# HGRN2's intra-chunk levels 1 to 32: products over the odd-block positions only, one masked copy per level, masks stored as bytes

## Chip, cores and metric

The kernel runs on one core of a Trainium2 chip. The metric is the device time of one execution in microseconds, as the median of several runs; less is better.

## What is computed

One decoder layer over 1024 prompt positions and 32 sampled positions (8 sequences of 4): RMS norm, one input projection, two mixers side by side (four mLSTM heads and four HGRN2 heads of 128 x 128), an output projection, a SwiGLU feed-forward block and a final norm. The change lies in the HGRN2 mixer, whose reference is

```
def _hgrn_chunk(S, inp):
    q, k, lf, v = inp
    b = jnp.cumsum(lf, axis=2)
    inter = jnp.einsum('bhtk,bhkv->bhtv', q * jnp.exp(b), S)
    dec = jnp.exp(jnp.where(mask[:, :, None], b[:, :, :, None, :] - b[:, :, None, :, :], -jnp.inf))
    A = jnp.einsum('bhtk,bhsk,bhtsk->bhts', q, k, dec)
    o = inter + jnp.einsum('bhts,bhsv->bhtv', A, v)
    S_new = jnp.exp(bL[:, :, 0, :])[..., None] * S + jnp.einsum('bhsk,bhsv->bhkv', k * jnp.exp(bL - b), v)
```

The matrix A couples a later position t with an earlier position s through a product of per-channel forget factors between them. The kernel works with chunks of 128 positions and builds A by levels, so that no quotient of factors is needed.

## The kernel before

**Stages.** The 1056 positions are cut into three blocks (288, 384 and 384 columns; the first holds 256 prompt positions and the 32 sampled ones). For each weight tile the input projection runs over the blocks: a unit is eight k-steps of three matmuls (`emit_k`, L135 to L137: high part times high part, low times high, high times low, with operands rounded for the fast matmul). Four units make one head of one block: first all mLSTM heads, then all HGRN2 heads, then the output projection and the feed-forward part.

**Order.** The program is written under a manual schedule: each engine executes its instructions in the order in which the Python code issues them, and semaphores hold an instruction until its inputs are there. Mixers are generators; `hook()` is called after every second k-step of a unit and lets each active generator run to its next `yield`, whose number says how many hooks to skip. So the mixer's small matmuls stand between k-steps of the projection on TensorE (PE), and its elementwise work stands in the queues of VectorE (DVE), ScalarE (ACT) and GpSimd (POOL) between the evacuation of projection results and the splitting of weights (L96 on ACT, L97 on POOL).

**One HGRN2 head of one block** is `mix_b(h, b)`: twelve times in all, with two chunks in block 0 and three in blocks 1 and 2. Channels lie on the partitions, positions along the free axis. `q`, `k` and the forget factors `f` are fp32 tiles (`cq`, `ck`, `ngb`); `qp` (tile `qw`) starts as q times f.

- Diagonal: one 128 x 128 product per chunk (`prod`, L757) goes to a PSUM bank; four multiplications by the identity, one per quadrant of 32 partitions (L772), copy the diagonal into AT, the tile that holds A transposed (s on the partitions, t along the free axis, one 128-column slice per chunk).
- Levels 1, 2, 4, 8, 16, 32, 64: at level l, t lies in the odd block of l positions and s in the even block before it. The products of `k` and `qp` are taken (levels 1 to 16: the whole 128 x 128 product per chunk, L757; level 32: two 32 x 32 products per chunk, L788; level 64: one 64 x 64 product, L793), then the odd blocks of `qp` are multiplied by the factors of the even block (DVE, L801), the even blocks of `k` by those of the odd block (POOL, L802), and pairs of factors are combined for the next level (DVE, L806). The wanted entries are copied out of PSUM: levels 1 to 8 by four masked copies of 32 partitions each (L813), level 16 by four plain copies (L821), levels 32 and 64 by ScalarE (L825, L827).
- Then k and v are transposed, the state is advanced, and AT times v and `qp` times the state make the output.

Block 0 also has the 32 sampled positions of the head: products of 32 x 32 (L759) at the diagonal and at levels 1 and 2, copied into tile PB (L776, L818). They use one quarter of the PE array's columns (`tile_position`).

AT is one of two tiles used in turn. The mLSTM gates of block 0 use the same two tiles as scratch, and `gates_sample` fills them with zeros on POOL when it is done (L391). The masks are part of the constant input: `cst` arrives as fp32 by one DMA on ACT's queue (L1615), and DVE converts the 64 mask columns to bytes (L1678) into tile `msk`.

An fp32 product is executed as two passes, each a weight load (PEld) and a matmul (PE) in the trace: 160 products of L757 in the levels show as 320 rows.

Of the kernel before, what the change touches and what calls it, by code (L numbers as in the profile page):

```python
# [9 lines left out]
F32 = mybir.dt.float32  # L10
F32R = mybir.dt.float32r
U8 = mybir.dt.uint8
AF = mybir.ActivationFunctionType
OP = mybir.AluOpType

D = 1024
T = 1056
# [14 lines left out]
NPLAIN = 2  # L32
EPS = 1e-6
QS = 128 ** -0.5
LEVELS = [1, 2, 4, 8]

V_G1, V_G2, V_GF, V_BIN, V_BG, V_CW, V_CB, V_MN, V_HN, V_LB, NV = 0, 8, 16, 24, 56, 57, 89, 97, 101, 105, 113

# [2 lines left out]
def hybrid_step(ctx: ExitStack, tc: tile.TileContext, i, o):  # L41
    nc = tc.nc
# [5 lines left out]
    mp = p1.enter_context(tc.tile_pool(name="mixp", bufs=1))  # L48
# [99 lines left out]

    vec = cn.tile([128, NV], F32, name="vec")
    ident = cn.tile([128, 128], F32, name="ident")  # L150
    cst = mp.tile([128, 232], F32, name="cst")
    msk = mp.tile([128, 64], U8, name="msk")
    X = act.tile([128, KT, T], F32, tag="X", name="X")
    x2 = [X]
    HI = act.tile([128, KT * T], F32R, name="HI")
# [22 lines left out]
    load_x(0)  # L178
    nc.scalar.dma_start(vec, i["vec"])
    maskneg, seqm, mneg4 = cst[:, 0:128], cst[:, 128:136], cst[:, 136:168]  # L180
    mk = {1: msk[:, 0:16], 2: msk[:, 16:32], 4: msk[:, 32:48], 8: msk[:, 48:64]}
    nc.scalar.preload_act_table_set("sqrt_and_others")
    ones = cn.tile([128, 1], F32, name="ones")
    nc.vector.memset(ones, 1.0)
# [168 lines left out]
    def gates_sample(ig, lf):  # L353
        def t5(name):
            return mp.tile([4, 40], F32, tag=name, name=name)

        def v5(x):
            return x.rearrange("p (s t) -> p s t", t=5)

        def s4(x):  # L360
            return x[:, 256:288].rearrange("p (s t) -> p s t", t=4)
        lfe, ige, rm, Fe, me = (t5(x) for x in ("lfe", "ige", "rme", "Fe", "me"))
        nc.vector.memset(lfe, -1e30)
        nc.vector.memset(rm, 1.0)
# [12 lines left out]
        nc.vector.tensor_tensor(wi, ng, m0s[:, :, None].to_broadcast([4, 8, 4]), op=OP.add)  # L377
        nc.scalar.activation(wi, wi, AF.Exp)
        nc.vector.tensor_tensor(wl, g, ng[:, :, 3:4].to_broadcast([4, 8, 4]), op=OP.add)
        nc.scalar.activation(wl, wl, AF.Exp)  # L380
        yield 2
        mo = mp.tile([4, 8], F32, tag="mso", name="mso")
        nc.vector.tensor_copy(mo[:, :, None], m4[:, :, 3:4])
        nc.sync.dma_start(o["ms"], mo)
        nc.sync.dma_start(d_sc.rearrange("j h t -> h j t"), r[:, 0:3].rearrange("p j s t -> p j (s t)"))
        nc.sync.dma_start(d_bc[:, 0, 256:288], ng.rearrange("p s t -> p (s t)"))
        nc.sync.dma_start(d_bc[:, 1, 256:288], wi.rearrange("p s t -> p (s t)"))
        for j in range(3):
            nc.sync.dma_start(scol[:, j:j + 1], d_sc[j].rearrange("h t -> (h t)")[:, None])
        for a in ATs:  # L390
            nc.gpsimd.memset(a, 0.0)  # L391

    def bc_row(row, n):
        return bass.AP(tensor=row.tensor, offset=row.offset, ap=[[0, 128], [1, n]])
# [201 lines left out]
    PB = mp.tile([128, 128], F32, name="PB")  # L596
# [148 lines left out]
    def mix_b(h, b):  # L745
        ncb, npr, n = NCH[b], NPR[b], BL[b]
        q, f, k = S["qb", h, b], S["f", h, b], S["kb", h, b]
        AT = ATs[atn[0] % 2]
# [5 lines left out]
        def prod(ps, a, c_, lo=0):  # L754
            for c in range(ncb):
                s = slice(c * 128, c * 128 + 128)
                nc.tensor.matmul(ps[:, s], a[:, s], c_[:, s], start=True, stop=True)  # L757
            if lo:
                nc.tensor.matmul(ps[32 * h:32 * h + 32, 256:288], a[:, 256:288], c_[:, 256:288], start=True, stop=True,  # L759
                                 tile_position=(0, 32 * h))  # L760

        def quads(fn):
            for j in range(4):
                fn(slice(32 * j, 32 * j + 32))
        hs = slice(32 * h, 32 * h + 32)
        nc.gpsimd.tensor_tensor(qp[:, :n], q[:, :n], f[:, :n], op=OP.mult)
        yield 2
        ps = bank()
        prod(ps, k, q, samp)

        def dg(js):
            nc.vector.tensor_tensor(AT[js, :ncb, js], ps[js, :npr].rearrange("p (c t) -> p c t", t=128)[:, :, js],  # L772
                                    ident[js, None, js].to_broadcast([32, ncb, 32]), op=OP.mult)
        quads(dg)
        if samp:
            nc.vector.tensor_tensor(PB[hs, hs], ps[hs, 256:288], ident[hs, hs], op=OP.mult)  # L776
        yield 2
# [1 line left out]
        while lv < 128:  # L779
            sm = samp and lv <= 2  # L780
            nn = n if sm else npr
            ps = bank()
            if lv <= 16:
                prod(ps, k, qp, sm)
            elif lv == 32:
                for c in range(ncb):
                    for s0 in (0, 64):
                        nc.tensor.matmul(ps[s0:s0 + 32, c * 128:c * 128 + 32], k[:, c * 128 + s0:c * 128 + s0 + 32],  # L788
                                         qp[:, c * 128 + s0 + 32:c * 128 + s0 + 64], start=True, stop=True,
                                         tile_position=(0, s0))  # L790
            else:
                for c in range(ncb):
                    nc.tensor.matmul(ps[0:64, c * 128:c * 128 + 64], k[:, c * 128:c * 128 + 64],  # L793
                                     qp[:, c * 128 + 64:c * 128 + 128], start=True, stop=True)
            nb = nn // (2 * lv)

# [7 lines left out]
            if lv == 4:  # L804
                go2 = go + nn // lv
            nc.vector.tensor_tensor(gx[:, go2:go2 + nb, None], gv[:, :, 0:1], gv[:, :, 1:2], op=OP.mult)  # L806
            pc = ps[:, :npr].rearrange("p (c t) -> p c t", t=128)
            if lv <= 8:
                def ext(js):
                    src = pc[js, :, js].rearrange("p c (n two l) -> p c n two l", two=2, l=lv)[:, :, :, 1, :]  # L810
                    dst = AT[js, :ncb, js].rearrange("p c (n two l) -> p c n two l", two=2, l=lv)[:, :, :, 1, :]
                    m = mk[lv][js].rearrange("p (n l) -> p n l", l=lv)
                    nc.vector.copy_predicated(dst, m[:, None].to_broadcast([32, ncb, 16 // lv, lv]), src)  # L813
                quads(ext)
                if sm:
                    src = ps[hs, 256:288].rearrange("p (n two l) -> p n two l", two=2, l=lv)[:, :, 1, :]
                    dst = PB[hs, hs].rearrange("p (n two l) -> p n two l", two=2, l=lv)[:, :, 1, :]
                    nc.vector.copy_predicated(dst, mk[lv][hs].rearrange("p (n l) -> p n l", l=lv), src)  # L818
            elif lv == 16:
                for j in range(4):  # L820
                    nc.vector.tensor_copy(AT[32 * j:32 * j + 16, :ncb, 32 * j + 16:32 * j + 32],  # L821
                                          pc[32 * j:32 * j + 16, :, 32 * j + 16:32 * j + 32])
            elif lv == 32:
                for s0 in (0, 64):
                    nc.scalar.activation(AT[s0:s0 + 32, :ncb, s0 + 32:s0 + 64], pc[s0:s0 + 32, :, 0:32], AF.Copy)  # L825
            else:
                nc.scalar.activation(AT[0:64, :ncb, 64:128], pc[0:64, :, 0:64], AF.Copy)  # L827
            if samp and lv == 2:
# [783 lines left out]

    load(0)
    nc.scalar.dma_start(ident, i["cst"][:, 0:128])
    nc.scalar.dma_start(cst, i["cst"][:, 128:360])  # L1615
    load(1)
    load(2)
    load_x(1)
# [56 lines left out]
    start(startup(1), ("n1", 1))  # L1675
    start(startup(2), ("n1", 2))
    hook()
    nc.vector.tensor_copy(msk, cst[:, 168:232])  # L1678
    nxt = 2
    b0_first = 3 + 12 * H  # L1680
    def next_splits(ui):
# [156 lines left out]

def _constants():
    p = np.arange(128)  # L1840
    cst = np.zeros((128, 360), np.float32)
    cst[:, 0:128] = np.eye(128)
    cst[:, 128:256] = np.where(p[:, None] <= p[None, :], 0.0, -1e30)
    cst[:, 256:264] = (p[:, None] % 32) // 4 == np.arange(8)[None, :]
    s, t = (p % 32)[:, None], np.arange(32)[None, :]
    cst[:, 264:296] = np.where((s // 4 == t // 4) & (s <= t), 0.0, -1e30)
    msk = cst[:, 296:360]
    r = p % 32
    for j, l in enumerate(LEVELS):
        n = np.arange(16) // l  # L1850
        msk[:, 16 * j:16 * j + 16] = ((r[:, None] // (2 * l)) == n[None, :]) & ((r[:, None] % (2 * l)) < l)
    return cst


def _prepare(x):
# [3 lines left out]
    def tiles(w):  # L1859
# [19 lines left out]
    xp = x["x_prompt"].reshape(1024, 1024)  # L1879
    xall = np.concatenate([xp[:256], x["x_sample"].reshape(32, 1024), xp[256:]], axis=0)  # L1880
    wgu = np.stack([tiles(x["w_gate"][0]), tiles(x["w_up"][0])], axis=1).reshape(44, 128, 1024)
    cst = _constants()
    return {
        "xT": xall.T.reshape(8, 128, T).transpose(1, 0, 2), "vec": vec, "cst": cst,
        "wA": wA, "wo": tiles(x["w_out"][0]), "wgu": wgu, "wd": x["w_down"][0],
        "hist": x["state_conv"][0].reshape(8, 3, 8, 128).transpose(3, 2, 0, 1).reshape(128, 8, 24),
        "C0": x["state_mlstm_C"][0], "n0T": x["state_mlstm_n"][0].transpose(2, 0, 1).reshape(128, 32),
# [28 lines left out]
```

## Time and profile before

| | |
|---|---|
| median of 3 runs | 1446.07 us (1445.78 to 1446.92) |
| the profiled execution's own time | 1442.34 us |
| its span | 1440.5 us |
| PE busy | 1366.2 us, 95% of the span |
| PE weight loads busy | 1334.2 us, 93% |
| DVE, ACT, POOL busy | 930.2 us (65%), 523.5 us (36%), 636.8 us (44%) |
| HGRN2 stage, from the first diagonal product to the last level | about 306 to 592 us of the span |

How to read it. The span is divided into stages whose limits differ, so the shares of the whole say little about one stage. PE is pipelined: a matmul's row lasts longer than the distance to the next one's start, and what a matmul costs in a dense stream is the distance from start to start. A row of the timeline that stands for several instructions (x6) begins with the first and ends with the last of them. An idle time in square brackets is the engine's, just before the row, with what ended it.

### The profile page before, as it was taken

Reading aid. Unit: us, or ns where it says so; the run is one execution under the profiler, and the core shown is the slowest. Engines: PE = TensorE matmul, PEld = TensorE weight load, DVE = VectorE, ACT = ScalarE, POOL = GpSimd, SP = SyncE. Lnnn points to the kernel's source line nnn. Section 1 sums busy time; section 2 is a strip of 40 time slices with the busy share of each in tenths; the row PEclk is TensorE's granted clock in tenths of the full one; section 3 lists DMA queues with packets and bytes.
Section 4 is the critical chain, followed back from the end, with each engine's and each line's share of the span. In section 5 each row is a group of like instructions: output and inputs, shape, how many; then the busy total and the mean of one; then the engine's idle time right before and its main releaser. Section 6 shows DMA issues by size and latency. Waiting matters only on the chain. (4 is left out here: it accounts for less than half of the span.)

```text
span 1440.5 us, 27183 instructions
## 1 busy us (share of the span) xinstructions
PE 1366.2 (95%) x10384; PEld 1334.2 (93%) x10384; DVE 930.2 (65%) x2192; ACT 523.5 (36%) x1195; POOL 636.8 (44%) x648
## 2 busy tenths in 40 slices
PE   7879999999999998999988998999999999999996
PEld 6779999999999998899988998999999999999995
DVE  7876657666777768744564655656555436777776
ACT  6554434322222223322434443444444441222232
POOL 5313213234343435222436654556545674544435
PEclk8999999999999999999999999999999999999998
DMA  6012212420101113553454655666565358887843
GB/s 218 23 42 76 65 37 73 123 80 30 33 30 32 45 32 112 144 155 105 158 196 146 217 210 167 216 220 220 193 212 186 124 190 333 291 298 277 300 157 121
DMA packets 108875, 211.97 MB, mean 147 GB/s; under 512 B 10800, under 2 KB 63560, under 8 KB 108232
## 3 DMA queue, kind: packets, MB, share of 16 engines
q1 hardware_dynamic: 108312, 209.98, 42.9%
q8 instruction: 82, 1.34, 0.4%
q14 instruction: 49, 0.40, 0.1%
q10 hardware_dynamic: 432, 0.24, 0.1%
HBM read 143.73 MB, written 66.45 MB: 146 GB/s over the span
## 5 line engine op out<-in xcount | busy, mean ns | idle before, releaser
L135 PE MATMUL mm<-HI,whi 128*128 128x384 f32 (+2 forms) x1160 | 381.9, 329 | 6.9 <-ACT gA L302 2.9
L136 PE MATMUL mm<-LO,whi 128*128 128x384 f32 (+2 forms) x1160 | 363.4, 313 | 0.9 <-POOL LO L225 0.4
L137 PE MATMUL mm<-HI,wlo 128*128 128x384 f32 (+2 forms) x1160 | 363.0, 313 | 1.3 <-POOL wlo L97 1.3
L135 PEld LDWEIGHTS mm<-HI,whi 128*128 128x128 f32 x1160 | 221.7, 191 | 12.0 <-ACT gA L302 3.2
L136 PEld LDWEIGHTS mm<-LO,whi 128*128 128x128 f32 x1160 | 221.9, 191 | 2.1 <-POOL LO L225 0.9
L137 PEld LDWEIGHTS mm<-HI,wlo 128*128 128x128 f32 x1160 | 221.5, 191 | 1.8 <-POOL wlo L97 1.8
L97 POOL TENSOR_TENSOR wlo<-raw,whi 128x512 fp32r<-128x512 f32 x90 | 119.8, 1340 | 143.8 <-ACT whi L96 98.8
L1365 DVE TENSOR_TENSOR fh<-fr,fh 128x512 fp32r<-128x512 f32 x80 | 71.6, 894 | 129.4 <-ACT fh L1364 129.3
L1157 POOL TENSOR_TENSOR wlo<-S,whi 128x512 fp32r<-128x512 f32 x78 | 103.2, 1328 | 115.9 <-ACT whi L1156 109.0
L1228 PE MATMUL mx<-T,whi 128*128 128x264 f32 x640 | 122.6, 290 | 12.4 <-DVE sg L1195 6.3
L1228 PEld LDWEIGHTS mx<-T,whi 128*128 128x128 f32 x640 | 101.7, 193 | 14.1 <-DVE sg L1195 7.3
L1281 POOL TENSOR_TENSOR LO<-rg,HI 128x528 fp32r<-128x528 f32 x52 | 70.5, 1365 | 65.7 <-ACT HI L1280 65.7
L1228 PE MATMUL mx<-HI,whi 128*128 128x264 f32 x320 | 91.7, 287 | 4.8 <-ACT u L1236 4.8
L1228 PE MATMUL mx<-T,wlo 128*128 128x264 f32 x320 | 92.3, 288 | 0.0
L1228 PE MATMUL mx<-HI,wlo 128*128 128x264 f32 x320 | 90.9, 284 | 0.0
L1228 PE MATMUL mx<-LO,whi 128*128 128x264 f32 x320 | 90.7, 284 | 0.0
L802 POOL TENSOR_TENSOR ck<-ck,wib 128x192 f32<-128x192 f32 (+2 forms) x72 | 41.3, 574 | 99.6 <-PE mx L757 56.1
L1156 ACT ACTIVATE whi<-S 128x512 fp32r<-128x512 f32 x80 | 50.4, 632 | 95.4 <-DVE S L1145 95.4
L1446 DVE TENSOR_TENSOR X<-X,mx 128x264 f32<-128x264 f32 x160 | 65.3, 424 | 27.1 <-PE mx L1442 26.6
L1364 ACT ACTIVATE fh<-fr 128x512 fp32r<-128x512 f32 x80 | 45.6, 572 | 71.5 <-issue 31.4
L1280 ACT ACTIVATE HI<-rg 128x528 fp32r<-128x528 f32 x52 | 32.3, 641 | 105.7 <-PE mx L1442 32.8
L1228 PE MATMUL mm<-HI,wlo 128*128 128x264 f32 x240 | 68.2, 284 | 0.0
(536 smaller groups left out, 3580.0 us busy)
## 6 DMA issues: line engine op xcount, KB each, us to landing
d_wf<-fh SPq DMA_DIRECT2D x60, 512.0 KB
rg<-d_ff SPq DMA_DIRECT2D x42, 528.0 KB
raw<-in_wA SPq DMA_DIRECT2D x31, 512.0 KB
whi<-d_wf SPq DMA_DIRECT2D x29, 512.0 KB
wlo<-d_wf SPq DMA_DIRECT2D x28, 512.0 KB
raw<-in_wgu SPq DMA_DIRECT2D x24, 512.0 KB
d_ff<-sg SPq DMA_DIRECT2D x40, 264.0 KB
rg<-in_wgu SPq DMA_DIRECT2D x20, 512.0 KB
```

The source lines that it names most:

```text
L97: (nc.gpsimd if pool else nc.vector).tensor_tensor(lo[:, s], raw[:, s], hi[:, s].bitcast(F32), op=OP.subtract)
L135: nc.tensor.matmul(ps[:, :n], wh, rh[:, k, :], start=(k == 0), stop=False)
L136: nc.tensor.matmul(ps[:, :n], wh, rl[:, k, :], start=False, stop=False)
L137: nc.tensor.matmul(ps[:, :n], wl, rh[:, k, :], start=False, stop=(k == nk - 1))
L802: nc.gpsimd.tensor_tensor(ke, ke, gv[:, :, 1:2].to_broadcast([128, nb, lv]), op=OP.mult)
L1156: nc.scalar.activation(hi[:, s], t, AF.Copy)
L1157: (nc.vector if dve else nc.gpsimd).tensor_tensor(lo[:, s], t, hi[:, s].bitcast(F32), op=OP.subtract)
L1228: nc.tensor.matmul(ps[:, :QN], a[:, w], b_[:, kk, c], start=new and kk == 0 and x == 0, stop=kk == 3 and x == 2, skip_group_check=True)
L1281: (nc.vector if dve else nc.gpsimd).tensor_tensor(lw, src, h.bitcast(F32), op=OP.subtract)
L1364: nc.scalar.activation(h, src, AF.Copy)
L1365: nc.vector.tensor_tensor(lw, src, h.bitcast(F32), op=OP.subtract)
L1446: nc.vector.tensor_tensor(y, y, ps[:, :QN], op=OP.add)
```

## The change

At levels 1 to 32 the moving operand of the product holds only the 64 positions of a chunk that lie in odd blocks (`odd(qp, l)`: runs of l positions with gaps of l), against all 128 columns of `k`, so each product is 128 x 64 and a level's result fills 64 columns per chunk in PSUM without gaps. At levels 1 to 16 one masked copy over 128 partitions and 64 positions per chunk takes the entries (level 16 now with a mask too); the diagonal is one multiplication over the whole 128 x 128 tile, which also writes the zeros, and so the fill of the two AT tiles goes. Level 32 has one product per chunk in place of two small ones; ScalarE copies as before, from other columns. Level 64 differs only in where its result lies in PSUM. The masks are 64 columns for each of the five levels, come as bytes by a DMA of their own on ACT's queue, and the conversion on DVE goes.

```diff
-LEVELS = [1, 2, 4, 8]
+LEVELS = [1, 2, 4, 8, 16]
...
-    cst = mp.tile([128, 232], F32, name="cst")
-    msk = mp.tile([128, 64], U8, name="msk")
+    cst = mp.tile([128, 168], F32, name="cst")
+    msk = mp.tile([128, 320], U8, name="msk")
...
-        for a in ATs:
-            nc.gpsimd.memset(a, 0.0)
...
-        def quads(fn):
-            for j in range(4):
-                fn(slice(32 * j, 32 * j + 32))
+        def odd(x, l):
+            return x.rearrange("p (n two l) -> p n two l", two=2, l=l)[:, :, 1, :]
+
+        def prod_odd(ps, l, lo):
+
+            for c in range(ncb):
+                s = slice(c * 128, c * 128 + 128)
+                nc.tensor.matmul(ps[:, 64 * c:64 * c + 64].rearrange("p (n l) -> p n l", l=l), k[:, s], odd(qp[:, s], l),
+                                 start=True, stop=True)
+            if lo:
+                nc.tensor.matmul(ps[32 * h:32 * h + 32, 256:288], k[:, 256:288], qp[:, 256:288], start=True, stop=True,
+                                 tile_position=(0, 32 * h))
...
-        def dg(js):
-            nc.vector.tensor_tensor(AT[js, :ncb, js], ps[js, :npr].rearrange("p (c t) -> p c t", t=128)[:, :, js],
-                                    ident[js, None, js].to_broadcast([32, ncb, 32]), op=OP.mult)
-        quads(dg)
+        nc.vector.tensor_tensor(AT[:, :ncb, :], ps[:, :npr].rearrange("p (c t) -> p c t", t=128),
+                                ident[:, None, :].to_broadcast([128, ncb, 128]), op=OP.mult)
...
-            if lv <= 16:
-                prod(ps, k, qp, sm)
-            elif lv == 32:
-                for c in range(ncb):
-                    for s0 in (0, 64):
-                        nc.tensor.matmul(ps[s0:s0 + 32, c * 128:c * 128 + 32], k[:, c * 128 + s0:c * 128 + s0 + 32],
-                                         qp[:, c * 128 + s0 + 32:c * 128 + s0 + 64], start=True, stop=True,
-                                         tile_position=(0, s0))
+            if lv <= 32:
+                prod_odd(ps, lv, sm)
...
-            if lv <= 8:
-                def ext(js):
-                    src = pc[js, :, js].rearrange("p c (n two l) -> p c n two l", two=2, l=lv)[:, :, :, 1, :]
-                    dst = AT[js, :ncb, js].rearrange("p c (n two l) -> p c n two l", two=2, l=lv)[:, :, :, 1, :]
-                    m = mk[lv][js].rearrange("p (n l) -> p n l", l=lv)
-                    nc.vector.copy_predicated(dst, m[:, None].to_broadcast([32, ncb, 16 // lv, lv]), src)
-                quads(ext)
+            if lv <= 16:
+                dst = AT[:, :ncb, :].rearrange("p c (n two l) -> p c n two l", two=2, l=lv)[:, :, :, 1, :]
+                m = mk[lv].rearrange("p (n l) -> p n l", l=lv)
+                nc.vector.copy_predicated(dst, m[:, None].to_broadcast([128, ncb, 64 // lv, lv]),
+                                          pc.rearrange("p c (n l) -> p c n l", l=lv))
...
-            elif lv == 16:
-                for j in range(4):
-                    nc.vector.tensor_copy(AT[32 * j:32 * j + 16, :ncb, 32 * j + 16:32 * j + 32],
-                                          pc[32 * j:32 * j + 16, :, 32 * j + 16:32 * j + 32])
...
-    nc.scalar.dma_start(cst, i["cst"][:, 128:360])
+    nc.scalar.dma_start(cst, i["cst"][:, 128:296])
+    nc.scalar.dma_start(msk, i["msk"])
...
-    nc.vector.tensor_copy(msk, cst[:, 168:232])
```

No other instruction changes its place on its engine.

## Rows read from the trace of the kernel before

**Rows 1.** Windows: stretch, length, busy us (instructions) of PE, PEld, DVE, ACT, POOL, clock, DMA

```profile
306.00:592.00 286.00, 279.60 (x2077) 266.36 (x2076) 209.28 (x651) 78.55 (x213) 119.23 (x165) 1.00 0.17 50
```

**Rows 2.** Timeline of PE around one level's six passes: start us, duration us, instruction

```profile
331.58 0.34 PE L137 MATMUL mm<-HI,wlo 128*128 128x384 f32 x1
331.75 0.83 PE L757 MATMUL mx<-qw,ck 128*128 128x128 f32 x6
...
332.60 0.34 PE L136 MATMUL mm<-LO,whi 128*128 128x384 f32 x1
```

**Rows 3.** Timeline of PE around six passes with one moving column (a norm's sums)

```profile
36.01 0.29 PE L137 MATMUL mx<-HI,wlo 128*128 128x288 f32 x1
36.14 0.73 PE L207 MATMUL mx<-ones,vt 128*128 128x1 f32 x6
...
36.94 0.29 PE L136 MATMUL mx<-LO,whi 128*128 128x288 f32 x1
```

**Rows 4.** Timeline of PE around level 32 of a three-chunk block

```profile
346.47 0.34 PE L137 MATMUL mm<-HI,wlo 128*128 128x384 f32 x1
346.74 0.38 PE L788 MATMUL mx<-qw,ck 128*32 128x32 f32 x12
...
347.33 0.34 PE L136 MATMUL mm<-LO,whi 128*128 128x384 f32 x1
```

**Rows 5.** Timeline of PE at level 2 of block 0, head 0

```profile
312.60 0.61 PE L757 MATMUL mx<-qw,ck 128*128 128x128 f32 x4
313.14 0.25 PE L759 MATMUL mx<-qw,ck 128*32 128x32 f32 x2
```

**Rows 6.** DVE groups by shape, 306 to 596 us: count, busy us, mean ns, idle before

```profile
L813 DVE COPY_PREDICATED AT<-msk,mx 32x48 f32<-32x48 uint8 x128 | 29.7, 232 | 3.2
L813 DVE COPY_PREDICATED AT<-msk,mx 32x32 f32<-32x32 uint8 x64 | 13.1, 205 | 1.5
L772 DVE TENSOR_TENSOR AT<-mx,ident 32x96 f32<-32x96 f32 x32 | 8.1, 254 | 12.8 <-PE mx L757 12.0
L821 DVE COPY AT<-mx 16x48 f32<-16x48 f32 x32 | 6.5, 202 | 0.7
L848 DVE COPY kt<-mx 128x384 f32<-128x384 f32 x7 | 3.9, 558 | 0.2
```

**Rows 7.** Timeline of PE, 550 to 593 us: rows with idle time before them

```profile
557.41 0.38 PE L788 MATMUL mx<-qw,ck 128*32 128x32 f32 x12 [1.97 <-DVE wib L806]
564.43 0.43 PE L672 MATMUL so<-st,qz 128*32 128x128 f32 x8 [1.81 <-DMA st<-in_S]
583.32 0.43 PE L672 MATMUL so<-st,qz 128*32 128x128 f32 x8 [0.43 <-POOL qz L633]
585.46 0.94 PE L757 MATMUL mx<-qw,ck 128*128 128x128 f32 x6 [0.42 <-POOL ck L802]
591.38 0.56 PE L793 MATMUL mx<-qw,ck 128*64 128x64 f32 x6 [0.97 <-POOL ck L802]
```

**Rows 8.** Timeline of DVE ahead of the first of these waits

```profile
550.86 0.93 DVE L813 COPY_PREDICATED AT<-msk,mx 32x48 f32<-32x48 uint8 x4
...
555.25 1.42 DVE L741 TENSOR_SCALAR ngb<-ngb,omlb,lb 128x384 f32<-128x384 f32 x1
```

**Rows 9.** Timeline of POOL ahead of the waits at 583 and 591 us

```profile
581.44 1.40 POOL L498 TENSOR_TENSOR sm<-sm,mhalf 128x3 f32<-128x3 f32 x1 [1.19 <-DVE sm L493]
...
590.10 0.60 POOL L498 TENSOR_TENSOR sm<-sm,mhalf 128x1 f32<-128x1 f32 x1 [2.56 <-DVE sm L493]
```

**Rows 10.** Timeline of DVE at the start of the program

```profile
27.01 1.26 DVE L1678 CAST msk<-cst 128x64 uint8<-128x64 f32 x1
...
31.31 1.22 DVE L1637 TENSOR_TENSOR vt<-vt,qw 128x384 f32<-128x384 f32 x2
32.64 3.02 DVE L1637 TENSOR_TENSOR vt<-vt,go 128x384 f32<-128x384 f32 x2
```

**Rows 11.** Page, part 3, DMA queue: packets, MB, share of 16 engines

```profile
q1 hardware_dynamic: 108312, 209.98, 42.9%
```

More of the change, by code (lines that the diff above doesn't have):

```diff
@@ L180, in hybrid_step @@
     maskneg, seqm, mneg4 = cst[:, 0:128], cst[:, 128:136], cst[:, 136:168]
-    mk = {1: msk[:, 0:16], 2: msk[:, 16:32], 4: msk[:, 32:48], 8: msk[:, 48:64]}
+    mk = {l: msk[:, 64 * j:64 * j + 64] for j, l in enumerate(LEVELS)}
     nc.scalar.preload_act_table_set("sqrt_and_others")
@@ L782, in mix_b @@
             ps = bank()
-            if lv <= 16:
-                prod(ps, k, qp, sm)
-            elif lv == 32:
-                for c in range(ncb):
-                    for s0 in (0, 64):
-                        nc.tensor.matmul(ps[s0:s0 + 32, c * 128:c * 128 + 32], k[:, c * 128 + s0:c * 128 + s0 + 32],
-                                         qp[:, c * 128 + s0 + 32:c * 128 + s0 + 64], start=True, stop=True,
-                                         tile_position=(0, s0))
+            if lv <= 32:
+                prod_odd(ps, lv, sm)
             else:
                 for c in range(ncb):
-                    nc.tensor.matmul(ps[0:64, c * 128:c * 128 + 64], k[:, c * 128:c * 128 + 64],
+                    nc.tensor.matmul(ps[0:64, c * 64:c * 64 + 64], k[:, c * 128:c * 128 + 64],
                                      qp[:, c * 128 + 64:c * 128 + 128], start=True, stop=True)
@@ L806, in mix_b @@
             nc.vector.tensor_tensor(gx[:, go2:go2 + nb, None], gv[:, :, 0:1], gv[:, :, 1:2], op=OP.mult)
-            pc = ps[:, :npr].rearrange("p (c t) -> p c t", t=128)
-            if lv <= 8:
-                def ext(js):
-                    src = pc[js, :, js].rearrange("p c (n two l) -> p c n two l", two=2, l=lv)[:, :, :, 1, :]
-                    dst = AT[js, :ncb, js].rearrange("p c (n two l) -> p c n two l", two=2, l=lv)[:, :, :, 1, :]
-                    m = mk[lv][js].rearrange("p (n l) -> p n l", l=lv)
-                    nc.vector.copy_predicated(dst, m[:, None].to_broadcast([32, ncb, 16 // lv, lv]), src)
-                quads(ext)
-                if sm:
-                    src = ps[hs, 256:288].rearrange("p (n two l) -> p n two l", two=2, l=lv)[:, :, 1, :]
-                    dst = PB[hs, hs].rearrange("p (n two l) -> p n two l", two=2, l=lv)[:, :, 1, :]
-                    nc.vector.copy_predicated(dst, mk[lv][hs].rearrange("p (n l) -> p n l", l=lv), src)
-            elif lv == 16:
-                for j in range(4):
-                    nc.vector.tensor_copy(AT[32 * j:32 * j + 16, :ncb, 32 * j + 16:32 * j + 32],
-                                          pc[32 * j:32 * j + 16, :, 32 * j + 16:32 * j + 32])
+            pc = ps[:, :64 * ncb].rearrange("p (c t) -> p c t", t=64)
+            if lv <= 16:
[3 more added lines that the diff above has]
+                                          pc.rearrange("p c (n l) -> p c n l", l=lv))
+                if sm:
+                    nc.vector.copy_predicated(odd(PB[hs, hs], lv),
+                                              mk[lv][hs, 16 * h:16 * h + 16].rearrange("p (n l) -> p n l", l=lv),
+                                              odd(ps[hs, 256:288], lv))
             elif lv == 32:
                 for s0 in (0, 64):
-                    nc.scalar.activation(AT[s0:s0 + 32, :ncb, s0 + 32:s0 + 64], pc[s0:s0 + 32, :, 0:32], AF.Copy)
+                    nc.scalar.activation(AT[s0:s0 + 32, :ncb, s0 + 32:s0 + 64], pc[s0:s0 + 32, :, s0 // 2:s0 // 2 + 32],
+                                         AF.Copy)
             else:
@@ L1840, in _constants @@
     p = np.arange(128)
-    cst = np.zeros((128, 360), np.float32)
+    cst = np.zeros((128, 296), np.float32)
     cst[:, 0:128] = np.eye(128)
@@ L1846, in _constants @@
     cst[:, 264:296] = np.where((s // 4 == t // 4) & (s <= t), 0.0, -1e30)
-    msk = cst[:, 296:360]
-    r = p % 32
+    msk = np.zeros((128, 64 * len(LEVELS)), np.uint8)
     for j, l in enumerate(LEVELS):
-        n = np.arange(16) // l
-        msk[:, 16 * j:16 * j + 16] = ((r[:, None] // (2 * l)) == n[None, :]) & ((r[:, None] % (2 * l)) < l)
-    return cst
+        n = np.arange(64) // l
+        msk[:, 64 * j:64 * j + 64] = ((p[:, None] // (2 * l)) == n[None, :]) & ((p[:, None] % (2 * l)) < l)
+    return cst, msk
 def _prepare(x):
@@ L1881, in _prepare @@
     wgu = np.stack([tiles(x["w_gate"][0]), tiles(x["w_up"][0])], axis=1).reshape(44, 128, 1024)
-    cst = _constants()
+    cst, msk = _constants()
     return {
-        "xT": xall.T.reshape(8, 128, T).transpose(1, 0, 2), "vec": vec, "cst": cst,
+        "xT": xall.T.reshape(8, 128, T).transpose(1, 0, 2), "vec": vec, "cst": cst, "msk": msk,
         "wA": wA, "wo": tiles(x["w_out"][0]), "wgu": wgu, "wd": x["w_down"][0],
```

## The prediction

> **What bounds the kernel now.** I read the windows first, then PE's timeline in the stage, then the rows that carry an idle time, and only then the groups of DVE, where most of the change lies. [...] DVE is three quarters full, but what it saves is worth something only where PE waits for it. Two questions follow: what does a product of 64 moving columns cost in PE's stream, and how much of the 6.4 us in which PE is idle goes away.
>
> **The cost of a pass.** An fp32 product is two passes. What a group of passes costs is how far it pushes the projection's matmuls apart. Six passes of 128 x 128 stand between L137 at 331.58 and the second matmul behind them at 332.60 [rows 2]: 1.02 us, of which L137 and L135 themselves take 2 x 0.17 (331.58 to 331.75). That leaves 0.68 us, 0.113 per pass. Now the same with one moving column: six passes of L207 stand between 36.01 and 36.94, 0.93 us less 2 x 0.13, again 0.67 us, 0.112 per pass [rows 3]. 128 moving columns and one cost the same: the pass is bounded by loading the 128 columns of the stationary operand. The changed products keep those (all of `k`) and halve only the moving side, which is not what a pass waits for. I therefore price a pass of 128 x 64 at 0.112, and the 320 passes of levels 1 to 16 at a change of zero. The ends would be 0.112 and half of it, 0.056; I take the upper, since 64 columns lie between the two counts that were seen to cost the same.
>
> [...]
>
> **The sum, part by part.**
>
> 1. Level 32. Twelve short passes now take 347.33 - 346.47 - 2 x 0.17 = 0.52 us, drains included [rows 4]. They become six passes with 128 stationary columns, 0.68 us. Eight units of three chunks: 8 x 0.16 = **+1.3 us**. The four units of block 0 go from eight short passes to four of 0.112 (0.45); I take them as even.
> 2. Levels 1 and 2 of block 0. The sampled product uses another part of the array and begins only when the last full pass has run out: 313.14 - 312.60 is 0.54, where four passes of 0.112 make 0.45, and the last of them alone more than a pass [rows 5]. A last pass of 64 columns runs out at most half a pass sooner: 8 places x 0 to 0.056. I take **-0.4 us** (0 to -0.45).
> 3. DVE. Each unit of three chunks has 16 masked copies of 232 ns, four copies of 202 and four diagonal multiplications of 254 [rows 6], 5.5 us. A masked copy of 192 elements is not in the trace. From 32 to 48 elements it grows by 27 ns, 1.7 per element: 232 + 144 x 1.7 = 477 ns. Towards the 558 ns of the 384-element copy the slope is 0.97: 372 ns. I take 430, between two ends that lie close; five of them make 2.15 us, and the diagonal (384 elements) 0.56. So a unit goes from 5.5 to 2.7, and twelve units save about 33 us of DVE. This is hidden behind PE and is priced at zero, except at the five waits of the next point.
> 4. PE's waits late in the stage [rows 7]. At 557.41 (1.97 us) DVE is late; from 550 us on it hardly pauses, and in that run is one group of masked copies (0.93, which becomes 0.43) and L741, which took 1.42 us beside a POOL instruction [rows 8]. I take -0.5; it can be -0.3 to -1.97, the latter if L741 gets ahead of POOL. At 564.43 a state load is late behind loads that wait for DVE: -0.3 (0 to -0.5, no more, since the load takes its own time). At 583.32 POOL is late because L498 waited 1.19 us for DVE's L493, which stood behind a group of masked copies [rows 9]: half a microsecond sooner closes it, -0.43. At 585.46 POOL follows on the same chain: -0.3 (0 to -0.42). At 591.38 POOL waited 2.56 us for DVE again, behind the four copies of level 16: -0.5 (0 to -0.97). Sum **-2.0 us** (bounds -0.3 and -4.3). What is late next is PE itself.
> 5. The start. DVE loses the conversion of the masks, 1.26 us at 27 us [rows 10]. Its next work is a chain of sums in which one takes 0.61 us alone and about 1.5 where POOL works beside it (31.31 and 32.64, two each), so coming earlier may only mean waiting for POOL: **-0.2 us** (bounds 0 and -1.3). The byte masks are one more DMA of 128 rows, eight packets per DMA engine; at the mean packet time of the main queue, 0.429 x 16 x 1440.5 / 108312 = 0.09 us [rows 11], that is at most +0.7, and I take it as hidden, since the first squares wait for X anyway. Its issue on ACT's queue lies in the same wait. The fill of the AT tiles leaves POOL at a time when PE does not wait for POOL: zero.
>
> Sum: 1.3 - 0.4 - 2.0 - 0.2 = **-1.3 us**. Against the profiled execution (1442.34 us) that is 1441.0. That execution was 3.7 us faster than the median of the runs, so I carry the difference over: 1446.1 - 1.3 = **1444.8 us**. The extremes of the terms are 1.3 - 0.45 - 4.3 - 1.3 = -4.8 and 1.3 - 0 - 0.3 + 0.7 = +1.7.
>
> **The rivals.** A measurement of this kernel tells a change from none above about 0.2%, 2.9 us.
>
> - A, the forecast: PE's stream is unchanged, some waits close, -2.9 to +1.7 us. Chance 0.56.
> - B: the waits close nearly fully and the start gains its microsecond, -2.9 to -4.8 us, 1441.3 at the end. For it: all five waits of rows 7 have DVE in their past, and DVE loses 33 of 209 us. Against it: three of them go through POOL, whose own work is not shortened, and the state load has its own time. Chance 0.25.
> - C: the passes do get shorter with their moving side. At half price, 320 x 0.056 = 17.9 us less, and level 32 loses nothing: about 1426. Against it stands the one-column group of rows 3. Chance 0.04.
> - D, slower: the moving operand now has gaps, at levels 1 and 2 after every one or two numbers. No row has such an operand. If reading it costs over twice what contiguous columns cost, the reading, and not the load, bounds the pass: that is the point from which it decides, 64 columns in over 0.112 us, 1.75 ns each. At double the pass, two levels of 64 passes give 128 x 0.112 = +14.3 us, about 1459. Against it: 64 positions over 128 columns, read at the rate of all 128, still fit in the pass that rows 2 show. Chance 0.07. [...]
> - E, slower: DVE and POOL meet differently. Where they collide a sum of 0.61 us takes 1.5 [rows 10]. If four new collisions of 0.9 us land on PE's path and none of the old waits closes, the time is 1446.1 + 1.3 - 0.4 + 3.6 = 1450.6. From three on it decides against me. Chance 0.08.
>
> **How the numbers follow.** The predicted time is A's, 1444.8. The range goes from B's end to A's upper end, 1441.3 to 1447.8, and 0.6 further on each side, since the runs shown lie within that of their median: 1440.7 to 1448.4. C, D and most of E stay outside, under 0.2. Faster is B and C, 0.29; slower D and E, 0.15; within 0.2% A, 0.56.
>
> **What would show it.** Six passes at a level should still push the stream apart by 0.67 to 0.68 us, with 64 columns in the row; if it is 0.35, C is right, if levels 1 and 2 show over 0.8, D. Level 32 should read 0.68 instead of 0.52. DVE's busy time should fall by 25 to 40 us. The masked copies should take 370 to 480 ns. PE's idle time between 550 and 593 us should be about two microseconds less. The prediction is wrong if PE's busy time in the stage moves by more than two microseconds, or if waits that DVE does not end appear.

## The result, and the profile after

| | before | after |
|---|---|---|
| median, first comparison (6 runs each) | 1446.49 us | 1437.07 us |
| ratio, 95% interval | | 0.9935 [0.9916, 0.9954] |
| ratio in two later comparisons (5 and 11 runs, beside 29 and 27 of the kernel before) | | 0.9965 [0.9953, 0.9977] and 0.9960 [0.9946, 0.9974] |
| the profiled execution's own time (span) | 1442.34 us (1440.5) | 1437.56 us (1435.7) |

The change makes the kernel faster by 5 to 9 us (1439.53 against 1444.66 in the last comparison, 1437.07 against 1446.49 in the first). The forecast was 1.3 us, and 1437 lies below its range. The 9.4 us of the first comparison did not come back: the two later ones show 5.7 and 5.1 us by their medians, and what follows explains these.

**The HGRN2 stage** did about what was forecast. First PE's timeline of the kernel after, in three places: a level of block 0 with its sampled product, a level of a three-chunk unit, and level 32 of such a unit.

```profile
311.97 0.29 PE L137 MATMUL mm<-HI,wlo 128*128 128x288 f32 x1
312.10 0.55 PE L767 MATMUL mx<-qw,ck 128*128 128x64 f32 x4
312.58 0.25 PE L770 MATMUL mx<-qw,ck 128*32 128x32 f32 x2
...
313.00 0.29 PE L136 MATMUL mm<-LO,whi 128*128 128x288 f32 x1
...
333.39 0.34 PE L137 MATMUL mm<-HI,wlo 128*128 128x384 f32 x1
333.56 0.78 PE L767 MATMUL mx<-qw,ck 128*128 128x64 f32 x6
...
334.40 0.34 PE L136 MATMUL mm<-LO,whi 128*128 128x384 f32 x1
...
348.35 0.34 PE L137 MATMUL mm<-HI,wlo 128*128 128x384 f32 x1
348.52 0.78 PE L767 MATMUL mx<-qw,ck 128*128 128x64 f32 x6
...
349.37 0.34 PE L136 MATMUL mm<-LO,whi 128*128 128x384 f32 x1
```

The second group pushes the projection apart by 334.40 - 333.39 - 2 x 0.17 = 0.67 us, as six passes of 128 and of one column did [rows 2, 3]. Half the moving columns save nothing. Level 32 reads 349.37 - 348.35 - 0.34 = 0.68 where it was 0.52 [rows 4]. In block 0 the sampled product starts 0.48 us behind the first pass and not 0.54 [rows 5].

DVE's groups by shape, 306 to 596 us of the kernel after (the columns of [rows 6]), and the window of the stage (those of [rows 1]):

```profile
L809 DVE COPY_PREDICATED AT<-msk,mx 128x192 f32<-128x192 uint8 x40 | 17.8, 444 | 0.0
L809 DVE COPY_PREDICATED AT<-msk,mx 128x128 f32<-128x128 uint8 x20 | 6.9, 345 | 0.0
L777 DVE TENSOR_TENSOR AT<-mx,ident 128x384 f32<-128x384 f32 x8 | 4.5, 558 | 11.7 <-PE mx L755 11.7
```

```profile
306.00:592.00 286.00, 282.61 (x2027) 272.79 (x2027) 175.81 (x436) 79.06 (x214) 120.69 (x166) 1.00 0.17 50
```

A masked copy of 192 columns takes 444 ns (I had taken 430), and DVE loses 209.3 - 175.8 = 33.5 us in the stage. PE's waits late in the stage, where five stood before [rows 7]:

```profile
565.29 0.43 PE L670 MATMUL so<-st,qz 128*32 128x128 f32 x8 [1.69 <-DMA st<-in_S]
588.20 0.85 PE L767 MATMUL mx<-qw,ck 128*128 128x64 f32 x6 [0.46 <-DVE wib L804]
591.35 0.56 PE L791 MATMUL mx<-qw,ck 128*64 128x64 f32 x6 [0.44 <-POOL ck L800]
```

5.60 us of waits have become 2.59. Counted between the same two projection matmuls (at 275.0 and 635.9 us of the kernel before), the stage takes 360.9 us before and 359.0 after.

**But the profiled time came from elsewhere.** In the one execution profiled, the kernel after had lost about as much before the stage began (the matmul at 275.0 us of the kernel before comes at 276.9; in a later trace of the same program, at 275.2). So both kernels enter the gate/up part of the feed-forward stage, which no line of the change touches, at the same time. These are the first gate/up matmul and the first matmul of the down product behind it, before (L1228, L1483) and after (L1221, L1476):

```profile
746.03 0.28 PE L1228 MATMUL mx<-HI,whi 128*128 128x264 f32 x1
...
1186.77 0.32 PE L1483 MATMUL mm<-HI,whi 128*128 128x352 f32 x1
```

```profile
746.02 0.28 PE L1221 MATMUL mx<-HI,whi 128*128 128x264 f32 x1
...
1182.86 0.32 PE L1476 MATMUL mm<-HI,whi 128*128 128x352 f32 x1
```

440.7 us against 436.8: of the 4.8 us between the spans of this pair 3.9 arise here. The same instructions stand there in the same order. PE's waits in this stretch, 740 to 1187 us, before and then after (who waited and for whom: us in total, times, longest):

```profile
PE mx L1228 <- DVE sg L1195: 6.3, 5, 3.5
PE mm L1228 <- ACT nt L1236: 6.1, 1, 6.1
PE mx L1228 <- DVE u L1201: 6.1, 3, 5.3
PE mx L1228 <- ACT u L1236: 4.8, 6, 1.3
```

```profile
PE mm L1221 <- ACT nt L1229: 5.8, 1, 5.8
PE mx L1221 <- DVE sg L1188: 5.4, 4, 3.8
PE mx L1221 <- DVE u L1194: 4.7, 2, 4.6
PE mx L1221 <- ACT u L1229: 3.5, 5, 1.2
```

23.3 us against 19.4. Why these waits shrink is what the experiments had to find.

### The profile page after: what moved, and what is told of

The parts are those of the page before. It is cut to its first block, busy times and chain, and to the rows that moved or that the text cites. A ratio compares the mean times of both kernels' runs of the same rounds, so it can differ in the third digit from the quotient of the medians.

```text
span 1435.7 us, 26848 instructions
## 1 busy us (share of the span) xinstructions
PE 1371.1 (95%) x10320; PEld 1343.2 (94%) x10320; DVE 891.2 (62%) x1975; ACT 524.2 (37%) x1195; POOL 636.2 (44%) x646
## 5 line engine op out<-in xcount | busy, mean ns | idle before, releaser
L97 POOL TENSOR_TENSOR wlo<-raw,whi 128x512 fp32r<-128x512 f32 x90 | 119.4, 1335 | 146.1 <-ACT whi L96 101.3
L1221 PE MATMUL mx<-T,whi 128*128 128x264 f32 x640 | 122.1, 290 | 10.3 <-DVE sg L1188 5.4
L1221 PEld LDWEIGHTS mx<-T,whi 128*128 128x128 f32 x640 | 101.5, 193 | 12.0 <-DVE sg L1188 6.5
L1221 PE MATMUL mx<-HI,whi 128*128 128x264 f32 x320 | 91.9, 287 | 3.5 <-ACT u L1229 3.5
L1221 PE MATMUL mx<-T,wlo 128*128 128x264 f32 x320 | 92.3, 288 | 0.0
L1221 PE MATMUL mx<-HI,wlo 128*128 128x264 f32 x320 | 90.9, 284 | 0.0
L1221 PE MATMUL mx<-LO,whi 128*128 128x264 f32 x320 | 90.8, 284 | 0.0
L1221 PE MATMUL mm<-HI,wlo 128*128 128x264 f32 x240 | 68.2, 284 | 0.0
```

The costliest lines, as they stand in the source:

```text
L97: (nc.gpsimd if pool else nc.vector).tensor_tensor(lo[:, s], raw[:, s], hi[:, s].bitcast(F32), op=OP.subtract)
L1221: nc.tensor.matmul(ps[:, :QN], a[:, w], b_[:, kk, c], start=new and kk == 0 and x == 0, stop=kk == 3 and x == 2, skip_group_check=True)
```

## First experiments: which part of the change?

Each takes one part of the change away or does one alone. The texts were written with two theories in mind: that the gain comes from DVE's relief in the mixer stage and the rest of the difference between the two traces is chance, or that the new constants (another tensor, another DMA) move it. All four ran beside the kernel before (1444.10 us, 29 runs). Here and below, differences in us are those of the medians; the ratios with their intervals are the recorded ones and are not exactly the quotients of the medians (they differ by up to 0.0008). `after_again` is the changed kernel once more.

> The changed kernel once more, for its spread and a second trace. Theory 1 (the gain comes from DVE's relief in the mixer stage, the rest of the difference between the two traces, 4.6 us behind 700 us, is chance): a median of 1439 to 1443 us, a time from run to run that moves by several us in the feed-forward stage, and PE idle there between 28 and 33 us. Theory 2 (the new mask input changes where tensors lie or how the first transfers go, and that speeds the feed-forward stage up): 1435 to 1439 again, PE idle there near 28 us again.

1438.44 us, 0.9965 [0.9953, 0.9977]. `const_only` is the kernel before with the masks as bytes from a DMA of their own and no conversion on DVE:

```diff
-    nc.scalar.dma_start(cst, i["cst"][:, 128:360])
+    nc.scalar.dma_start(cst, i["cst"][:, 128:296])
+    nc.scalar.dma_start(msk, i["msk"])
...
-    nc.vector.tensor_copy(msk, cst[:, 168:232])
```

> The kernel before with the constants of the changed one: shorter cst, byte masks by a DMA of their own, no conversion on DVE; products and copies as before. Theory 1: within 1.5 us of before, 1445 to 1447. Theory 2: most of the gain, 1438 to 1441, with PE idle behind 640 us down from 32.7 to about 28 us and the stage from 306 to 592 as before.

1443.83 us, 1.0001 [0.9987, 1.0015]. The constants show no worth; the interval is some 2 us to either side. `copies` keeps the changed kernel's copies but multiplies as before (`prod` at levels 1 to 16, two 32 x 32 products at level 32):

```diff
-            if lv <= 32:
-                prod_odd(ps, lv, sm)
+            if lv <= 16:
+                prod(ps, k, qp, sm)
+            elif lv == 32:
...
```

> The changed kernel with the products of before: 128 x 128 at levels 1 to 16, two of 32 x 32 at level 32. Only DVE's copies, the diagonal and the constants are new. Both theories: 0.5 to 1.5 us faster than the changed kernel, since level 32 costs PE 0.16 us per three-chunk unit there and the 64-column passes give nothing back. If the halved moving side did give something, it would be slower than the changed kernel instead.

1440.64 us, 0.9977 [0.9964, 0.9990]: not 0.5 to 1.5 us below the changed kernel, but 2.2 above it. `old32` is the changed kernel with the old products at level 32 alone:

```diff
-            if lv <= 32:
+            if lv <= 16:
                 prod_odd(ps, lv, sm)
+            elif lv == 32:
...
```

> The changed kernel with the two 32 x 32 products of before at level 32. Six passes fewer by 0.16 us in eight units: 1.3 us faster than the changed kernel, 1435.8 if that is at 1437.1. If ACT's copies, which get their input later with the long product, were on a path that PE waits for, more.

1442.24 us, 0.9990 [0.9976, 1.0004]. This was the surprise: without its dearest part, the longer level 32, the kernel was slower than with it by 3.8 us. In the traces of const_only, copies and old32 PE idles 32 to 33 us behind the HGRN2 stage, as before; in both traces of the changed kernel 28. What old32 has and the changed kernel lacks is 64 passes on PE.

## A new theory: where PE's instructions are fetched

The page's instruction counts and DMA queues, before and then after (engines: busy us, share, instructions; queues: packets, MB, share):

```profile
PE 1366.2 (95%) x10384; PEld 1334.2 (93%) x10384; DVE 930.2 (65%) x2192; ACT 523.5 (36%) x1195; POOL 636.8 (44%) x648
...
q8 instruction: 82, 1.34, 0.4%
```

```profile
PE 1371.1 (95%) x10320; PEld 1343.2 (94%) x10320; DVE 891.2 (62%) x1975; ACT 524.2 (37%) x1195; POOL 636.2 (44%) x646
...
q8 instruction: 81, 1.33, 0.4%
```

1.34 MB over 2 x 10384 PE instructions is some 64 bytes each, so queue 8 carries PE's code, and a packet of 16 KB (1.34 MB in 82) holds 256 instructions. Each took 0.88 to 2.45 us, 1.01 at the median. In the feed-forward stage (746 to 1180 us of the kernel before) one comes every 17 us on average, 13.5 to 24.3. The change takes 64 weight loads and 64 matmuls out of the stream (level 32 has one product per chunk for two), 128 instructions: half a packet. So behind the HGRN2 stage the fetches fall about half an interval elsewhere: those at 981.20 and 999.07 us come at 988.11 and 1004.81 in the kernel after, while the loads they stood at come 2.5 and 3.1 us earlier. In the kernel before one falls on the issue of a weight load. The DMA queues in 999.0 to 999.6 us of that kernel, then its SP, ACT and PE rows (start, us, instruction, idle before):

```profile
q8 instruction: 1, 0.02, 12.4%
```

```profile
999.12 1.51 SPq L1357 DMA_DIRECT2D fr<-in_wd  x1
...
1004.53 0.63 ACT L1364 ACTIVATE fh<-fr 128x512 fp32r<-128x512 f32 x1 [1.38 <-DMA fr<-in_wd]
...
1015.68 0.51 PE L1228 MATMUL mx<-T,whi 128*128 128x264 f32 x2 [0.58 <-DVE u L1201]
```

The same three of the kernel after, where no packet of queue 8 is near:

```profile
996.00 0.43 SPq L1350 DMA_DIRECT2D fr<-in_wd  x1
...
1000.90 0.63 ACT L1357 ACTIVATE fh<-fr 128x512 fp32r<-128x512 f32 x1 [0.87 <-DMA fr<-in_wd]
...
1012.11 0.52 PE L1221 MATMUL mx<-T,whi 128*128 128x264 f32 x2 [0.15 <-DVE u L1194]
```

The issue takes 1.51 us instead of 0.43, and ACT has the 512 KB load 5.41 us after it instead of 4.90. ACT and DVE split these weights in order with the work that PE waits for. In the kernel before, the down-weight loads at 981, 999 and 1033 us have a fetch at their issue (0.03 to 0.13 us ahead of it) and the one at 1016 has it 2.7 us later; in the kernel after none of the four has.

The test is to move the fetches and nothing else: 32 dummy products of one column, 128 PE instructions, put where PE waits anyway. `before_pad32` puts them into the 3.7 us wait of the first mLSTM head, into unused columns of its bank:

```diff
+            if (h, b, c) == (0, 0, 1):
+                for _ in range(32):
+                    nc.tensor.matmul(pO_[0:1, 400:401], vt[:, 0, 0:1], vt[:, 0, 0:1], start=True, stop=True)
             nc.tensor.matmul(pO[:, c, 0:129], W[:, s], vt[:, c, 0:129], start=True, stop=cin[c] is None)
```

> The kernel before with 32 dummy one-by-one fp32 products (64 passes, 128 PE instructions) issued at 81 us, where PE waits 3.7 us for DVE; nothing else differs. Theory I (position of PE's instruction stream: the trace shows PE's instruction fetches as 16 KB packets, one per 256 instructions of 64 bytes; the change shortens the stream by 128 instructions, half a packet, and every kernel measured so far with FF idle time of 32 to 33 us has its fetches at one set of places and both of 28 us at the other): the same half packet is shifted here, so the time falls by about 4 us against before (ratio 0.9965 to 0.998), with PE idle in the feed-forward stage near 28 us. Theory L (level 32's new product, through what it does in the mixer stage): ratio 1.000, feed-forward idle 32 to 33 us. Theory N (runs of one program scatter by 4 us and the difference was chance): ratio 1.000.

1439.78 us against 1444.43, **0.9974 [0.9960, 0.9988]**: adding work to the kernel before makes it 4.6 us faster. PE's idle time behind the HGRN2 stage was 30.9 us. `before_pad64` has 64 of them, a whole packet:

> The same with 64 dummy products (128 passes, 256 PE instructions, one whole packet): prices the dummies themselves. All theories: ratio 1.000 to 1.0015 (64 more passes of some 30 to 60 ns, mostly in the 3.7 us wait), feed-forward idle 32 to 33 us. If it too falls by 4 us, the dummies act by something else than the place of the fetches (the clock at 81 us, for one).

1443.40 us, 0.9996 [0.9983, 1.0009], idle 34.3 us. The dummies as such do nothing that is clear of the noise. `after_pad32` puts the 32 into the changed kernel:

> The changed kernel with the 32 dummy products at the same place: PE's stream is as long as before from there on to the HGRN2 stage and has the old place of its fetches after it. Theory I: 4 us slower than the changed kernel, ratio 0.999 to 1.001 against before, feed-forward idle 32 to 33 us. Theories L and N: as the changed kernel was, 0.9955 to 0.9975, idle 28 us (L), or anything between (N).

1441.52 us, 0.9985 [0.9971, 0.9998], idle 32.2 us: about half of the gain is gone, since 2.9 us are left where the changed kernel had 5.7 and 5.1 in its later comparisons. Theory I had expected all 4 us back. `new32` changes only level 32 of the kernel before (and where ScalarE reads it):

```diff
-                    for s0 in (0, 64):
-                        nc.tensor.matmul(ps[s0:s0 + 32, c * 128:c * 128 + 32], k[:, c * 128 + s0:c * 128 + s0 + 32],
...
+                    nc.tensor.matmul(ps[:, c * 128:c * 128 + 64].rearrange("p (n l) -> p n l", l=32), k[:, s],
+                                     qp[:, s].rearrange("p (n two l) -> p n two l", two=2, l=32)[:, :, 1, :],
+                                     start=True, stop=True)
```

> The kernel before with only level 32 changed (one 128x64 product per chunk in place of two of 32x32; 64 passes less), copies and constants as before. My prediction's own step says +1.3 us by PE's stream. Theory L: 3 to 4 us faster than before, ratio 0.997 to 0.998, feed-forward idle 28 us. Theory I: the same (its stream loses the same 128 instructions), less the waits that the change's DVE savings close: 0.997 to 0.999. Theory N: +1.3 us, 1.001.

1442.81 us, 0.9995 [0.9980, 1.0010], so neither theory's 0.997 to 0.999. Its trace has 28.1 us of idle behind the HGRN2 stage, as I and L both said, but in that one execution the HGRN2 stage takes 365.2 us, 4.3 more than before. By 549 us of the kernel before 1.5 of them are there, all at level 32; the state load that ends a wait of 1.81 us before ends one of 2.69 here; and 1.6 us are lost from 571.3 to 574.7 us, where the granted clock fell while PE was busy (its mean from 545 to 592 us is 0.96; 1.00 in the kernel before). Six other traces have such a fall as well (0.96 there, as here), but ahead of the wait for that load, and their stages are no longer than before's (360.5 to 361.1 us). So this run does not separate the theories.

## Where in the program it acts

`before_mid32` puts the 32 products at the head of the third gate/up step, at 757 us, where PE waits 5 to 6 us; all ahead of them is the kernel before:

```diff
+            if (u, p, j) == (0, "P5", 0):
+                for _ in range(32):
+                    nc.tensor.matmul(ps[0:1, 400:401], ident[:, 0:1], ident[:, 0:1], start=True, stop=True,
+                                     skip_group_check=True)
```

> The kernel before with the 32 dummy products (128 PE instructions) placed at 757 us, in PE's 5 to 6 us wait at the start of the feed-forward stage: everything up to there is the kernel before. Theory F (the change shortens PE's stream by half a packet of instruction fetch, and with the fetches at the old places four loads of the down weights, at 981, 999, 1016 and 1033 us, share the DMA engines with a 16 KB fetch and land 0.6 to 1.6 us late, where PE has no slack): the fetches move by half a packet from 757 us on, so as with the pad at 81 us: ratio 0.997 to 0.998, PE's waits at 973 and 1016 us (1.07 and 1.75 us in most traces) fall to about 0.2. Rival M (the pad at 81 us acted through the clock or the order in the mLSTM or HGRN2 stage): ratio 1.000, waits unchanged.

1438.68 us against 1443.96, **0.9968 [0.9952, 0.9984]**. The load, its use and PE's wait in its trace:

```profile
999.78 0.43 SPq L1361 DMA_DIRECT2D fr<-in_wd  x1
...
1004.85 0.63 ACT L1368 ACTIVATE fh<-fr 128x512 fp32r<-128x512 f32 x1 [1.04 <-DMA fr<-in_wd]
...
1015.98 0.51 PE L1232 MATMUL mx<-T,whi 128*128 128x264 f32 x2 [0.23 <-DVE u L1201]
```

`before_late32` has them at 1083 us (step `(14, "P4")`), behind the four loads. There they fall into a bank whose sums are still open, so part of those sums is not the reference's; every instruction still runs.

> The same 32 dummy products placed at 1083 us, in a wait of 3.5 us behind those four loads. Theory F: the loads at 981 to 1033 us still meet their fetches; ratio 0.9995 to 1.000 (the wait of 0.78 us at 1248 us may go), waits at 973 and 1016 us as before. A theory by which the length of the program or the number of instructions as such matters: 0.997 as with the other pads.

1445.19 us, 1.0009 [0.9993, 1.0025]. So what counts lies between 757 and 1083 us. `before_pad16` shifts by a quarter packet, with 16 dummies at 81 us:

> 16 dummy products at 81 us (64 PE instructions, a quarter packet): the fetches come some 4 us earlier against the loads. By the offsets in the traces (fetch -0.1 us from the issue of the loads at 981, 999, 1033 us, +2.7 at 1016, +3.5 at 947) they leave the first four and meet the load at 947 us. Theory F: ratio 0.997 to 0.999. Rival (only the half packet matters, by an alignment inside the stream): 1.000.

1442.05 us, 0.9987 [0.9975, 1.0000]: 1.9 us against the 4.6 of the half packet, with an interval that ends at no change. Its fetches leave the four loads and meet those at 929 and 947 us, which ACT now has 6.02 and 5.51 us after the issue instead of 4.5 and 4.4; PE's wait at 945 us grows from 0.55 to 1.61. `old32_pad32` combines the old level 32 with the pad at 81 us:

> The changed kernel with the old products of level 32 (twelve of 32x32 in a three-chunk unit) and the 32 dummy products at 81 us: the cheaper level 32 and the favourable place of the fetches together. Theory F: 3 to 4 us faster than without the pad (1442.2), ratio 0.996, at or 1.3 us below the changed kernel itself; feed-forward idle 28 to 29 us. Theory L (the new level 32 as such gives the time): 0.999 as without the pad.

1440.64 us, 0.9985 [0.9970, 1.0000]: better than old32 had been, by 1.6 us and not by 3 to 4, and not below the changed kernel. That left open what the change is worth by itself.

## The change's own part

Three kernels beside the kernel before (1444.66 us): the changed kernel, the same with the 32 dummies at 757 us, and old32 with them there.

> The changed kernel as it is, a third time, as the base of the next two. Theory F: 0.995 to 0.997 against before, feed-forward idle 28 us.

1439.53 us, 0.9960 [0.9946, 0.9974].

> The changed kernel with 32 dummy products at 757 us, in PE's wait at the start of the feed-forward stage: start, mLSTM and HGRN2 stages are the changed kernel's, only the fetches behind 757 us go back to the places of the kernel before. Theory F: 3 to 5 us slower than the changed kernel, 0.9985 to 0.9995 against before, the waits at 1016 and 1031 us are back (over 0.5 us each), feed-forward idle over 30 us; what is left against before, -1 to -2 us, is the change's own part in the HGRN2 stage. If the change's own work gives the time, it stays at 0.996.

1443.25 us, **0.9997 [0.9985, 1.0009]**: with all of the change in place and only the later fetches back where they were, it is 3.7 us slower than the changed kernel and 1.4 us faster than before, which the interval does not part from no change (by the ratios it is 5.3 and 0.4 us). The collision is back in its trace:

```profile
996.42 1.43 SPq L1354 DMA_DIRECT2D fr<-in_wd  x1
...
1003.12 0.63 ACT L1361 ACTIVATE fh<-fr 128x512 fp32r<-128x512 f32 x1 [2.68 <-DMA fr<-in_wd]
...
1014.24 0.69 PE L1225 MATMUL mx<-T,whi 128*128 128x264 f32 x2 [1.75 <-DVE u L1194]
```

The expected wait at 1031 us did not come back; those at 1016 and, at 0.52 us, 1053, which after_third lacks, did.

> The changed kernel with the old products of level 32 and the 32 dummy products at 757 us: the HGRN2 stage of old32 and the favourable fetches of the changed kernel from 757 us on. Theory F and level 32's price of +1.3 us: 1 to 2 us below the changed kernel, 0.995 to 0.996. If level 32's price is given back by a wait elsewhere: even with the changed kernel.

1440.82 us, 0.9969 [0.9953, 0.9984]: even with the changed kernel within the intervals (1.3 us above it by the medians), not 1 to 2 us below it. Between the two projection matmuls named above, the traces of the changed kernel with the old level 32 take 358.1 to 358.3 us and those with the new one 358.5 to 359.2, so of the 1.3 us about 0.7 shows. The traces show where the rest goes: at 590 us of the kernel before the two kinds are still 1.2 us apart on average, and the last wait, at level 64, which is 0.95 us in old32 and 0.44 in the changed kernel, gives 0.5 back. No kernel tried is clearly below the changed one.

The traces of all kernels fall into two groups by the place of the fetches, whatever else differs. With the four loads met (eight traces, among them before, old32 and after_mid32) PE's wait at 1016 us is 0.58 to 1.77 us; with them clear (nine) 0.14 to 0.53. PE's idle time ahead of all the matmuls that the kernel before runs from 950 to 1070 us sums to 3.6 to 7.1 us in the first group and to 1.4 to 2.9 in the second. The medians part less cleanly: copies, with the loads met, is at 0.9977, and new32, with them clear, at 0.9995.

What a met load costs shows best in the one at about 910 us. The trace has sixteen marks of landing for each load. In the nine traces without a fetch there the last mark comes 4.0 to 4.5 us after the issue; in the eight where a fetch starts 2.6 or 2.7 us after the issue it comes after 5.9 to 6.0, while the other fifteen are there by 4.0 to 4.6. So one of the load's sixteen parts is late, 1.3 to 1.9 us behind the rest, and ACT begins only behind it: 5.93 to 6.05 us after the issue, against 4.78 to 4.80 in the first group, where it comes straight from other work and has not waited. There PE has slack: in the first pair of traces it does not idle from 912 to 923 us.

## Why the prediction was wrong, point by point

- **The cost of a pass** was right: 0.67 us for six passes of 64 columns, with gaps of one or two numbers. With 128 stationary columns six passes took 0.67 or 0.68 us for 128, 64 and one moving column; twelve with 32 stationary columns took 0.52 [rows 2, 3, 4]. Rivals C and D are out.
- **Part 1, level 32**, +1.3: right in PE's stream (0.68), but the whole stage shows about 0.7, since the last wait gives 0.5 back. This is also the part where the prediction failed, below.
- **Part 2**, -0.4: right. Eight groups of block 0 lost 0.05 us each.
- **Part 3**, DVE: 33.5 us against some 33, hidden but for the waits.
- **Part 4, PE's waits**, -2.0: 5.60 - 2.59 = -3.0, within the bounds. The wait at 557 us closed fully, where I took a quarter of it; 583, 585 and 591 closed as forecast or a little more; a new one of 0.46 us appeared; the state load hardly moved (1.81 to 1.69). So 3.0 of 5.6 us closed, and with the stage 1.9 us shorter this is A and not yet B. E, new collisions of DVE and POOL, can at most be in the new wait: ahead of it DVE's L799 takes 1.27 us beside POOL's L97 (at 583 us), where the same work took 0.36 before (L801, at 582). The lower bound, -0.3, counted the wait at 583 us at nothing, though its -0.43 had been given no range.
- **The prediction's own sign**, PE's busy time in the stage moving by more than two microseconds, did appear: 282.61 - 279.60 = 3.0 us. But the window has a fixed length, so this is the 3.0 us of waits that closed, and not dearer work.
- **Part 5, the start**, -0.2: const_only shows nothing measurable, 1.0001. The DMA of the byte masks moved 144 packets (queue 10 has 576 of them after and 432 before), nine for each of the 16 engines where I counted eight.
- The sum, -1.3, agrees with what the runs show of the change's own work, but they show it loosely: after_mid32 gives -1.4 (its interval from -2.2 to +1.3), after_pad32 -2.9 (-4.2 to -0.3), the stage's length in the first pair of traces -1.9.
- The base and the margin came from three runs. One of them lies 0.85 us from their median and not within 0.6, and the 27 to 35 runs of each later comparison spread from 1437.5 to 1452.1 us around medians of 1444.0 to 1444.7, so the base of 1446.1 was 1.4 to 2.1 us high. Against the better base the changed kernel is still 5.1 and 5.7 us faster and not 1.3.
- **What failed** is the step that closed the account there. Part 1 ("Twelve short passes ... become six passes") priced the passes by PE's time alone, and the sum and the range took nothing but the terms of the start and of the HGRN2 stage, so the feed-forward stage was put at zero without a reason. The prediction left out that fewer instructions move every later instruction fetch, and that the feed-forward stage has waits that hang on single loads. The runs put 3.7 us (after_third against after_mid32) to 5.3 us (before_mid32 against before) there, or 5.3 and 4.6 by the ratios: more than the change's own part. The page lists the instruction queue and the counts, so the shift of half a packet could have been worked out, and a bound for it from the stage's waits. Its sign could not, without laying the fetches against the loads.

## What to carry to other kernels

When a change alters the number of instructions on the busiest engine, look at where its code is fetched, and compare stages that the change does not touch: a gain or loss there is not the change's own and can be given back by the next edit (here 3.7 of 5.1 us, after_mid32). Padding the stream with a few idle products, in a wait and by half a fetch packet, separated the two here; a whole packet of them is the control. Issuing such a load earlier, so that it is in time even where a fetch meets it, would be the next step; it was not tried.

## What was unexpected

PE's instruction fetch is visible as transfers of 16 KB (82 of them), and one that meets a 512 KB load delays its first use by about 1.2 us (4.79 to 6.0, at 910 us). When it falls on the issue (24 of the loads between 900 and 1060 us in all traces), the issue takes 1.19 to 1.68 us on SP; the 129 others take 0.39 to 0.46. The fetches are 0.4% of the DMA engines' time. The landing marks tell why so little costs so much: a fetch, of about 1 us, goes with the delay of a single one of the load's sixteen parts, and ACT waits for that part. Why the issue itself takes longer stays open.
